# A decoder trunk on one core: each dense product in seven block products, all tokens per stage

## The chip, the cores and the metric

One core of a Trainium2 chip (trn2) runs the whole program. The metric is device time in microseconds (us) of one execution; lower is better. The engines are TensorE (PE in the rows; PEld is its loading of weights), VectorE (DVE), ScalarE (ACT), Pool (GpSimd) and SyncE (SP), which issues every DMA in one queue.

## The reference, cut to what matters

The stream x has 1024 tokens of 1024 features, in float32. Layer 0 mixes tokens by a Conformer convolution, layer 1 by causal differential attention with 8 heads; both are followed by a gated FFN with a hidden width of 2816 and a causal convolution of width 3. Every sub-layer is wrapped in RMS norms and in shift, scale and gate vectors that are computed from c.

```python
u = h @ w1 + b1;  a, gt = split(u);  u = a * sigmoid(gt)             # layer 0
u = causal_dwconv(u, dw, dwb)                                        # 31 taps
y = silu(layer_norm(u)) @ w2 + b2
s = q @ k.T * scale + bias;  p = softmax(s)                          # layer 1, two maps a head
y = rms_norm((p[0] - lam * p[1]) @ v) @ w_o
u = causal_dwconv(h @ w_in, ffn_dw, ffn_dwb);  g, v = split(u)       # FFN, 3 taps
y = (silu(g) * v) @ w_out
x = x + gate * rms_norm(y)                                           # after each sub-layer
```

The dense products are w1 (1024 x 2048), w2, w_q, w_k, w_v, w_o (1024 x 1024 each), and for each of two FFNs w_in (1024 x 5632) and w_out (2816 x 1024).

## The kernel before, in words

Every operand of a product is kept as two float32r tiles, hi (the value rounded to float32r) and lo (what the rounding left), and a product of a 128 x 128 block is three matmuls: hi x hi, hi x lo, lo x hi. `featmm` (L206 to L214) gives a tile of 128 features by 512 tokens; `tokmm` (L216 to L251) gives four tiles of 128 tokens by 512 columns. `wsplit` (L173 to L193) loads a weight tile of 128 x 1024, copies hi on ScalarE (L191) and subtracts lo (L192), on Pool by a share that `plan['pool']` sets, otherwise on VectorE.

The 1024 tokens are worked in two halves, A and B, of 512. A planner written by hand, `interleave` (L72), runs one generator of the other half's work beside the steps of an FFN:

- The convolution of half A has its own time: 7 of 31 taps go through TensorE as products with a diagonal (L468), 24 are instructions of VectorE on PSUM (L473). The convolution of half B runs beside the FFN of half A (`interleave` at L645).
- Attention of half A (`attn`, L742 to L862) runs beside the FFN of layer 0 of half B (L919), and attention of half B beside the FFN of layer 1 of half A (L934).
- Residual sums, norms and transposes of one half (`residual` L299, `transposing` L275) are placed beside products of the other.

`ffn` (L389) makes w_in's products chunk by chunk, takes three taps from PSUM (L402, L405, L406), the gate (L415, L416), the operands (L168, L169), and after each of three parts of the hidden width adds w_out's products into y (L427). The activations between the two products stay in SBUF. The modulation vectors are 96 dot products of loaded tiles of 128 x 1024 (`mod_dot`, L341 to L345). In attention, each tile of 128 queries and each of two maps has scores (L788), bias and maximum on VectorE (L793, L800, L804), the exponential on ScalarE (L805), then the two maps are combined (L807 to L810), transposed (L827), rounded (L829, L830) and multiplied with V (L836 to L838); squares for the norm follow (L843 to L858).

Order within an engine is that of its queue. Tile buffers rotate in pools, and a load of a tile waits in SP's queue until a buffer is free, with all later DMAs behind it.

## Time and profile before

| | us |
|---|---|
| Two runs | 2617.18 and 2612.99, median 2615.09 |
| Profiled execution, first to last instruction (span) | 2617.6 |

The profile gives no time of its own execution beside the span. It names an engine, a line, an operation and tiles as output <- inputs. A busy time is that of a group of instructions, where an overlap counts once; a mean is that of one instruction. A matmul's own duration overlaps with the next one's, so TensorE's pace is read from the number of matmuls in a stretch. The granted clock is given as a share of 2.4 GHz.

### The profile page before, as it was taken

How to read it: one execution, taken by the hardware profiler on the slowest of the kernel's cores; microseconds unless marked ns; L12 is line 12 of the kernel's file. 1: busy time of each engine (PE TensorE's matmuls, PEld its weight loads, DVE VectorE, ACT ScalarE, POOL GpSimd, SP SyncE). 2: the span in 40 equal slices, each digit the busy share in tenths (PEclk: the TensorE clock that was granted, in tenths of full speed). 3: DMA queues.
4: the chain of work that ended last, by engine and by line, in shares of the span. 5: the costliest groups of instructions: out<-in, count | busy, mean ns of one | idle time of the engine just before them, and what ended most of it. 6: DMA issues, size and time to landing. Idle time of an engine off the chain costs nothing.

```text
span 2617.6 us, 30604 instructions
## 1 busy us (share of the span) xinstructions
PE 2442.6 (93%) x10678; PEld 1923.3 (73%) x10678; DVE 1768.1 (68%) x3289; ACT 1160.1 (44%) x1883; POOL 921.0 (35%) x487
## 2 busy tenths in 40 slices
PE   6998889999989979999999999999999998999997
PEld 4666667777767767787787778777777776788885
DVE  6998689999788438747667844775676665624335
ACT  4433234332444225647554533655664544433333
POOL 2234334544644322222222333323323334344443
PEclk9999989999999989999999999999999999999999
DMA  7123753443335877444453486445445324433332
GB/s 279 57 65 99 208 183 96 142 141 120 105 111 181 266 200 218 137 133 137 127 163 105 138 290 200 141 120 136 119 129 137 120 84 158 161 97 91 95 97 73
DMA packets 161898, 370.31 MB, mean 141 GB/s; under 512 B 21712, under 2 KB 70224, under 8 KB 161744
## 3 DMA queue, kind: packets, MB, share of 16 engines
q1 hardware_dynamic: 161744, 368.36, 46.0%
q8 instruction: 85, 1.39, 0.2%
q14 instruction: 69, 0.57, 0.1%
HBM read 320.56 MB, written 47.73 MB: 141 GB/s over the span
## 4 chain that ended last, share of the span: by engine, by line
PE 44%; DVE 14%; DMA 3%; issue 3%; ACT 2%; POOL 1%; SPq 0%; DVEq 0%; ACTq 0%; POOLq 0%
PE Pu L214 8%; PE Pu L212 8%; PE Pu L213 8%; PE Py L228 5%; PE Py L229 5%; PE Py L227 5%; PE Psc L788 2%; DMA mraw<-in_mw_dram 2%; DVE tap L405 1%; DVE p L810 1%; DVE tap L406 1%; DVE gT L169 1%; POOL wlo L192 1%; PE Ptr L827 1%; DVE tap L416 1%
## 5 line engine op out<-in xcount | busy, mean ns | idle before, releaser
L192 POOL TENSOR_TENSOR wlo<-raw,whi 128x1024 fp32r<-128x1024 f32 x344 | 843.7, 2453 | 1539.9 <-ACT whi L191 1453.7
L191 ACT CAST whi<-raw 128x1024 fp32r<-128x1024 f32 x374 | 392.2, 1049 | 665.2 <-issue 310.5
L212 PE MATMUL Pu<-hT,whi 128*128 128x512 f32 x1536 | 616.9, 402 | 18.5 <-DVE tap L406 11.1
L214 PE MATMUL Pu<-hT,wlo 128*128 128x512 f32 x1536 | 611.7, 398 | 3.2 <-POOL wlo L192 3.2
L213 PE MATMUL Pu<-hT,whi 128*128 128x512 f32 x1536 | 611.1, 398 | 1.0 <-DVE hT L290 0.9
L227 PE MATMUL Py<-whi,gT 128*128 128x512 f32 x960 | 387.2, 404 | 31.5 <-DVE hl L689 14.2
L228 PE MATMUL Py<-wlo,gT 128*128 128x512 f32 x960 | 385.0, 401 | 4.7 <-POOL wlo L192 4.6
L229 PE MATMUL Py<-whi,gT 128*128 128x512 f32 x960 | 383.5, 399 | 0.5 <-DVE gT L169 0.5
L212 PEld LDWEIGHTS Pu<-hT,whi 128*128 128x128 f32 x1536 | 291.5, 190 | 89.8 <-issue 15.9
L214 PEld LDWEIGHTS Pu<-hT,wlo 128*128 128x128 f32 x1536 | 291.3, 190 | 70.6 <-POOL wlo L192 5.2
L213 PEld LDWEIGHTS Pu<-hT,whi 128*128 128x128 f32 x1536 | 291.4, 190 | 65.8 <-DVE hT L290 2.4
L473 DVE SCALAR_TENSOR_TENSOR Pcv<-cu,sv,Pcv 128x512 f32<-128x512 f32 x432 | 299.7, 747 | 3.4 <-PE Pcv L468 2.5
L405 DVE SCALAR_TENSOR_TENSOR tap<-Pu,sv,tap 128x511 f32<-128x511 f32 x176 | 131.1, 745 | 199.8 <-ACT tap L402 169.8
L227 PEld LDWEIGHTS Py<-whi,gT 128*128 128x128 f32 x960 | 183.8, 191 | 75.6 <-issue 17.1
L228 PEld LDWEIGHTS Py<-wlo,gT 128*128 128x128 f32 x960 | 183.7, 191 | 47.7 <-POOL wlo L192 8.1
L229 PEld LDWEIGHTS Py<-whi,gT 128*128 128x128 f32 x960 | 183.4, 191 | 42.6 <-DVE gT L169 1.0
L345 DVE CUSTOM_DVE_ANT_0 mraw<-mraw,crow 128x1024 f32<-128x1024 f32 x96 | 147.5, 1538 | 74.1 <-DMA mraw<-in_mw_dram 74.0
L402 ACT ACTIVATE tap<-Pu,sv 128x512 f32<-128x512 f32 x176 | 136.2, 774 | 4.3 <-PE Pu L214 4.3
L406 DVE SCALAR_TENSOR_TENSOR tap<-Pu,sv,tap 128x510 f32<-128x510 f32 x176 | 130.9, 744 | 2.6
L168 ACT CAST gT<-tap 128x512 fp32r<-128x512 f32 x88 | 54.5, 619 | 162.2 <-DVE tap L416 162.0
L805 ACT ACTIVATE p<-p,sm 128x128 f32<-128x128 f32 (+7 forms) x128 | 99.2, 775 | 49.8 <-DVE sm L804 48.7
L169 DVE TENSOR_TENSOR gT<-tap,gT 128x512 fp32r<-128x512 f32 x88 | 89.5, 1018 | 31.6 <-ACT gT L168 31.0
(213 smaller groups left out, 3377.9 us busy)
## 6 DMA issues: line engine op xcount, KB each, us to landing
raw<-in_win_dram SPq DMA_DIRECT2D x176, 512.0 KB, 3.7
mraw<-in_mw_dram SPq DMA_DIRECT2D x96, 512.0 KB, 4.6
raw<-in_wout_dram SPq DMA_DIRECT2D x88, 512.0 KB, 3.7
raw<-in_w_dram SPq DMA_DIRECT2D x48, 512.0 KB, 3.7
Q<-qd SPq DMA_DIRECT2D x128, 128.0 KB, 3.3
K<-kd SPq DMA_DIRECT2D x48, 256.0 KB, 4.6
V<-vd SPq DMA_DIRECT2D x192, 64.0 KB, 2.0
xt<-xd SPq DMA_DIRECT2D x20, 512.0 KB, 4.9
```

The costliest lines, as they stand in the source:

```text
L191: A.copy(hi, raw)
L192: e.tensor_tensor(out=lo, in0=raw, in1=hi.bitcast(F32), op=ALU.subtract)
L212: T.matmul(ps, lhsT=a, rhs=ah, start=(k == 0), stop=False)
L213: T.matmul(ps, lhsT=a, rhs=al, start=False, stop=False)
L214: T.matmul(ps, lhsT=b, rhs=ah, start=False, stop=(k == KC - 1))
L227: T.matmul(ps[t], lhsT=a, rhs=rh, start=(f == 0), stop=False)
L228: T.matmul(ps[t], lhsT=a, rhs=rl, start=False, stop=False)
L229: T.matmul(ps[t], lhsT=b, rhs=rh, start=False, stop=(f == n - 1))
L345: V.tensor_tensor_reduce(out=raw, in0=raw, in1=crow, scale=1.0, scalar=0.0, op0=ALU.mult, op1=ALU.add, accum_out=r[:, k:k + 1])
L405: V.scalar_tensor_tensor(out=t[:, 1:512], in0=ps[:, 0:511], scalar=w[1], in1=t[:, 1:512], op0=ALU.mult, op1=ALU.add)
L406: V.scalar_tensor_tensor(out=t[:, 2:512], in0=ps[:, 0:510], scalar=w[0], in1=t[:, 2:512], op0=ALU.mult, op1=ALU.add)
L473: V.scalar_tensor_tensor(out=ps, in0=u[:, j:j + 512], scalar=col("dw", j * 8 + c), in1=ps, op0=ALU.mult, op1=ALU.add)
```

## The change

Each dense product C = A B is cut into 2 x 2 blocks and made from seven block products, of sums and differences of blocks of A and of B, with additions of the results. All 1024 tokens go through a stage before the next begins: the two halves of the tokens are the two block columns, so there is no second half to interleave with.

- `Feat` makes products that end with features on the partitions (w1, w_in, w_k, w_q). A step (q, p) is one of seven products for a pair of chunks q: `prep` forms its block of weights (four sums S per pair) and the hi and lo of it, `step` has 12 matmuls of 512 columns and one addition or copy of the result, and `ahead` prepares five steps early. Two steps of each of the first two pairs need the first token half alone and are made early. `w_k` and `w_q` are scaled, so that Q, K and V share one set of operands; Q's shift becomes a bias (`q_bias`).
- `token_stage` makes products that end with tokens on the partitions (w2, w_v, w_o, w_out). A step loads one block of activations and one of weights from HBM, 256 KB each, and splits each into hi and lo (`loaded`); in w_v the activations are the operands already there.
- Activations between two products and the sums of their blocks are stored in HBM (`prep_s`), as are sums of weight blocks (`prep_t`, `prep_v`).
- `eng` sends a share of the sums and subtractions to Pool: 0.9 in the convolution, 0.3 in `Feat`, 0.25 elsewhere.
- `operands_2` makes the operands' block sums once the second token half is there.
- The convolution (31 taps on 1024 tokens per chunk) runs in w1's stage: 7 taps on TensorE, 5 on ScalarE and Pool, 19 on VectorE. LayerNorm follows by itself, then w2.
- Attention runs by itself, both halves one after the other, between w_q and w_o. K, V and Q come in two sets of buffers, and PSUM is one pool of 8 banks.
- A `Ticker` spreads other work over the steps: the FFN's taps and gate, `prep_s` and `prep_t`, and the modulation vectors, 48 of whose dots go along with the down-projection of layer 0.

The core of the diff:

```diff
-P1, P2, P3, P4 = 1, 1, 0.7, 1      # share of the weights' lo parts made by Pool: convolution, Q/K/V, the two attention phases
-AE, BE = 52, 52      # FFN steps that attention goes along with, first and second half
...
+FEAT = (1, 6, 2, 5, 7, 3, 4)
+TOK = (1, 6, 2, 5, 3, 7, 4)
+BANK = {1: 0, 2: 0, 6: 1, 5: 2, 3: 2, 7: 3, 4: 3}
+OPEN = (1, 6, 5, 7)
+NHS, NWS, NSS, NQ = 56, 12, 6, 12
+LA = 5
+LAT = 4
...
+    def tick(self, n=1):
+        n += len(self.q) > 1
+        while n > 0 and self.q:
+            if next(self.q[0], "end") == "end":
+                self.q.popleft()
+            else:
+                n -= 1
...
+    def eng():
+        plan["debt"] += plan["pool"]
+        if plan["debt"] >= 1.0:
+            plan["debt"] -= 1.0
+            return G
+        return V
...
+    def operands_2(xn, scale, shift, H, Z):
+        for kp in range(4):
+            z = Z[kp]
+            zz = [s2("zz"), s2("zz")]
+            for two in range(2):
+                k = 2 * kp + two
+                ps = bank("Pt")
+                for t in range(4):
+                    T.transpose(ps[:, t * P:(t + 1) * P], xn[4 + t][:, k * P:(k + 1) * P], ident)
+                scaled(zz[two], ps, scale, shift, k)
+            def put(i, src):
+                pr = hpair()
+                split(*pr, src, eng())
+                H[i].append(pr)
+            sub(half(z, 0), zz[0], half(z, 0))
+            sub(zz[0], zz[1], zz[0])
+            put(3, zz[1])
+            sub(zz[1], zz[1], half(z, 0))
+            put(6, zz[1])
+            sub(half(z, 1), half(z, 1), zz[1])
+            put(5, half(z, 0))
+            put(7, zz[0])
+            put(4, half(z, 1))
+            yield
...
+        def __init__(self, n, src, H, done, ticks=1, scale=None):
+            self.n, self.src, self.H, self.done, self.ticks, self.scale = n, src, H, done, ticks, scale
+            e = min(EARLY, n)
+            self.steps = [(q, p) for p in (1, 2) for q in range(e)]
+            self.early = len(self.steps)
+            self.steps += [(q, p) for q in range(e) for p in FEAT if p not in (1, 2)]
+            self.steps += [(q, p) for q in range(e, n) for p in FEAT]
+            self.raw, self.sums, self.pairs, self.banks, self.outs = {}, {}, {}, {}, {}
+            self.at, self.made = 0, 0
...
+        def prep(self, q, p):
+            def a1(i):
+                return self.rawof(q, 0)[:, i]
+            def a2(i):
...
+            def s(n):
+                if n not in su:
+                    t = None
+                    if n == 1:
+                        t = s2("S")
+                        add(v4(t), a2(0), a2(1), eng())
+                    elif n == 2:
+                        a = s(1)
+                        t = s2("S")
+                        sub(v4(t), a, a1(0), eng())
+                    elif n == 3:
+                        t = s2("S")
+                        sub(v4(t), a1(0), a2(0), eng())
+                    else:
+                        a = s(2)
...
+            src = {1: lambda: a1(0), 2: lambda: a1(1), 3: lambda: s(4), 4: lambda: a2(1), 5: lambda: s(1), 6: lambda: s(2),
+                   7: lambda: s(3)}[p]()
+            hi, lo = wpair()
+            A.copy(v4(hi), src)
+            eng().tensor_tensor(out=v4(lo), in0=src, in1=v4(hi).bitcast(F32), op=ALU.subtract)
+            self.pairs[q, p] = hi, lo
...
+        def step(self):
+            q, p = self.steps[self.at]
+            hi, lo = self.pairs.pop((q, p))
+            b = BANK[p]
+            if p in OPEN:
+                self.banks[q, b] = bank("Pf")
+            ps = self.banks[q, b]
+            for j in range(4):
+                ah, al = self.H[p][j]
+                w, v = hi[:, j * P:(j + 1) * P], lo[:, j * P:(j + 1) * P]
+                more = {"skip_group_check": True} if b != 1 else {}
+                T.matmul(ps, lhsT=w, rhs=ah, start=(p in OPEN and j == 0), stop=False, **more)
+                T.matmul(ps, lhsT=w, rhs=al, start=False, stop=False, **more)
+                T.matmul(ps, lhsT=v, rhs=ah, start=False, stop=(j == 3), **more)
+            if p == 1:
+                self.outs[q] = [q4("X"), None]
+            o = self.outs[q]
+            if p == 6:
+                o[1] = q4("Y")
+            X, Y = o
+            if p == 1:
+                A.copy(half(X, 1), ps)
+            elif p == 6:
+                add(half(Y, 0), ps, half(X, 1))
+            elif p == 2:
+                A.copy(half(X, 0), ps)
+            elif p == 5:
+                add(half(Y, 1), ps, half(Y, 0))
+            elif p == 7:
+                add(half(Y, 1), ps, half(Y, 1))
+            elif p == 3:
+                add(half(X, 1), ps, half(Y, 0))
+            else:
+                add(half(Y, 0), ps, half(Y, 0))
+                self.tk.add(self.done(q, X, Y))
+            self.at += 1
...
+        def rest(self):
+            while self.at < len(self.steps):
+                self.ahead(self.at + 1 + LA)
+                self.step()
+                self.tk.tick(self.ticks)
+            self.tk.flush()
...
+    def prep_t(wsrc, dst, e=None):
+        u, v = q4("tu"), q4("tv")
+        dma(out=u, in_=wsrc(0))
+        dma(out=v, in_=wsrc(1))
+        yield
+        sub(half(u, 0), half(v, 0), half(u, 0), eng())
+        yield
+        sub(half(v, 0), half(v, 1), half(v, 0), eng())
+        yield
+        sub(half(v, 1), half(v, 1), half(u, 0), eng())
+        yield
+        sub(half(u, 1), half(u, 1), half(v, 1), eng())
+        dma(out=dst[0], in_=u)
+        dma(out=dst[1], in_=v)
...
+    def prep_s(g0, g1, dst):
+        dma(out=dst[0][:, 0:512], in_=half(g0, 0))
+        dma(out=dst[1], in_=g1)
+        a, b = s2("S"), s2("S")
...
+    def loaded(src, mk):
+        r = w2k("raw")
+        dma(out=r, in_=src)
+        pr = mk()
+        split(*pr, r, eng())
+        return pr
...
+        def ahead(upto):
+            while made[0] < min(upto, len(steps)):
+                p, j = steps[made[0]]
+                have[p, j] = asrc(p, j), bsrc(p, j)
+                made[0] += 1
...
+        def mm(p, j, t, ps):
+            (ah, al), (bh, bl) = have[p, j]
+            a, b = ah[:, t * P:(t + 1) * P], al[:, t * P:(t + 1) * P]
+            more = {"skip_group_check": True} if p != 6 else {}
+            T.matmul(ps[t], lhsT=a, rhs=bh, start=(p in OPEN and j == 0), stop=False, **more)
+            T.matmul(ps[t], lhsT=a, rhs=bl, start=False, stop=False, **more)
+            T.matmul(ps[t], lhsT=b, rhs=bh, start=False, stop=(j == n - 1), **more)
...
+        k = 0
+        for p in TOK:
+            if p in OPEN:
+                banks[BANK[p]] = [bank("Py") for _ in range(4)]
+            ps = banks[BANK[p]]
+            jm = n - late if p == TOK[-1] else n
+            for j in range(jm):
+                ahead(k + 1 + LAT)
+                for t in range(4):
+                    mm(p, j, t, ps)
+                have.pop((p, j))
+                k += 1
+                tk.tick(ticks)
+            if jm == n:
+                for t in range(4):
+                    evac(p, t, ps[t])
+            else:
+                ahead(len(steps))
+                for t in range(4):
+                    for j in range(jm, n):
+                        mm(p, j, t, ps)
+                    evac(p, t, ps[t])
+                    tk.tick(ticks)
...
+        def pre(t, nh):
+            a = half(y[t], nh)
+            if bt is not None:
+                add(a, a, bt[nh])
+            square(a, ss2[:, nh * 8 + t:nh * 8 + t + 1])
+            eng().tensor_tensor(out=a, in0=a, in1=gn[nh], op=ALU.mult)
+            yield
...
+        token_stage(n, asrc, bsrc, lambda t, nh: half(y[t], nh), fin, Both(), ticks, late=late)
+        tk.flush()
+        after.flush()
+        if nxt is not None:
+            if nxt[3] is not None:
+                nxt[3].begin()
+            drain(operands_2(y, nxt[0], nxt[1], nxt[2], Z))
...
+        onpe = list(range(0, NPE))
+        onpool = list(range(NPE, NPE + NPOOL))
+        onv = list(range(NPE + NPOOL, CW))
+        for d in onpe:
+            dg = big.tile([P, P], F32, tag="dg", bufs=3, name=nm("dg"))
+            A.activation(dg, ident, AF.Copy, scale=w(d))
+            last = d == onpe[-1]
+            T.matmul(ps[0][:, d:512], lhsT=dg, rhs=X[:, 0:512 - d], start=(d == 0), stop=last)
+            T.matmul(ps[1], lhsT=dg, rhs=X[:, 512 - d:1024 - d], start=(d == 0), stop=last)
...
+        def done(q, X, Y):
+            ts = []
+            for ch, src in ((q, X), (q + FC, Y)):
+                w = [col("fdw", (l * 3 + j) * 44 + ch) for j in range(3)]
+                t = q4("tap")
+                A.activation(t, src, AF.Identity, bias=col("fdwb", l * 44 + ch), scale=w[2])
+                yield
+                V.scalar_tensor_tensor(out=t[:, 1:], in0=src[:, 0:1023], scalar=w[1], in1=t[:, 1:], op0=ALU.mult, op1=ALU.add)
+                V.scalar_tensor_tensor(out=t[:, 2:], in0=src[:, 0:1022], scalar=w[0], in1=t[:, 2:], op0=ALU.mult, op1=ALU.add)
+                yield
+                ts.append(t)
+            tg, tv = ts
+            A.activation(tg, tg, AF.Silu)
+            yield
+            V.tensor_tensor(out=tv, in0=tg, in1=tv, op=ALU.mult)
+            if q % 2 == 0:
+                G0[q] = tv
+                yield from prep_t(lambda nh: wout[l, nh, q // 2], td[q // 2])
+            else:
+                yield from prep_s(G0.pop(q - 1), tv, ad[q // 2])
+        f = Feat(FC, lambda q: (win[l, q], win[l, q + FC]), H, done)
...
+    for g in (mod_scale(1, 1, 0, s_m1), mod_col(1, 0, sh_m1), gate_row(1, 2, 1, gd_m1), mod_scale(1, 4, 2, s_f1),
+              mod_col(1, 3, sh_f1), gate_row(1, 5, 3, gd_f1), *[prep_v(j) for j in range(4)],
+              *[prep_t(lambda nh, j=j: wo[nh, j], wot[j]) for j in range(4)]):
+        tk.add(g)
+    with_residual(FC // 2, fa0, fb0, gd_f0, lambda t: xd[0][t], lambda t: xd[1][t], (None, None, H, fk), tk, late=6)
+    plan["pool"] = WPOOL
+    fk.tk.add(strips())
+    fk.tk.add(q_bias())
+    fk.rest()
...
+    token_stage(4, lambda p, j: H[p][j], lambda p, j: loaded(sblock(wva[j], p), wpair), lambda t, nh: half(vy[t], nh), v_fin, vt,
+                transposed=True)
...
+    fq.begin_ahead()
+    fq.begin()
+    vt.flush()
+    fq.rest()
+    hopen.close()
...
+    drain(attn(0))
+    wo_norm(0)
+    drain(attn(1))
+    wo_norm(1)
...
+    for j in range(4):
+        drain(prep_s(wo_act(2 * j), wo_act(2 * j + 1), woa[j]))
+    aopen.close()
...
+    f1, fa1, fb1 = ffn(1, H)
+    with_residual(4, lambda p, j: loaded(sblock(woa[j], p), hpair), tok_weights(lambda nh, j: wo[nh, j], wot), gd_m1,
+                  lambda t: xd[1][t], lambda t: xd[2][t], (s_f1, sh_f1, H, f1), Ticker())
+    plan["pool"] = WPOOL
+    f1.rest()
+    plan["pool"] = TPOOL
+    with_residual(FC // 2, fa1, fb1, gd_f1, lambda t: xd[2][t], lambda t: out[t], None, Ticker(), late=6)
```

## Rows read from the trace of the kernel before

**Rows 1.** The page, busy time of each engine, share of the span, instructions.
```profile
PE 2442.6 (93%) x10678; PEld 1923.3 (73%) x10678; DVE 1768.1 (68%) x3289; ACT 1160.1 (44%) x1883; POOL 921.0 (35%) x487
```

**Rows 2.** The page, chain of work that ended last, by engine.
```profile
PE 44%; DVE 14%; DMA 3%; issue 3%; ACT 2%; POOL 1%; SPq 0%; DVEq 0%; ACTq 0%; POOLq 0%
```

**Rows 3.** Busy time by stretch: length, busy (instructions), clock, DMA share, GB/s.
```profile
130.00:196.00 66.00, 66.00 (x238) 44.45 (x237) 63.52 (x97) 23.11 (x49) 22.93 (x11) 1.00 0.22 64
...
1113.00:1178.00 65.00, 64.36 (x303) 52.08 (x302) 30.95 (x101) 30.47 (x63) 17.24 (x13) 1.00 0.49 134
...
2356.00:2421.00 65.00, 65.00 (x281) 52.69 (x281) 27.47 (x50) 23.00 (x29) 28.68 (x12) 1.00 0.30 90
```

**Rows 4.** Groups of instructions: busy us, mean ns, idle before and releaser.
```profile
L192 POOL TENSOR_TENSOR wlo<-raw,whi 128x1024 fp32r<-128x1024 f32 x344 | 843.7, 2453 | 1539.9 <-ACT whi L191 1453.7 <-DMA V<-vd 14.1 <-PE Pu L213 13.8
L212 PE MATMUL Pu<-hT,whi 128*128 128x512 f32 x1536 | 616.9, 402 | 18.5 <-DVE tap L406 11.1 <-DVE hT L289 1.9 <-ACT c L477 1.9
...
L473 DVE SCALAR_TENSOR_TENSOR Pcv<-cu,sv,Pcv 128x512 f32<-128x512 f32 x432 | 299.7, 747 | 3.4 <-PE Pcv L468 2.5
...
L345 DVE CUSTOM_DVE_ANT_0 mraw<-mraw,crow 128x1024 f32<-128x1024 f32 x96 | 147.5, 1538 | 74.1 <-DMA mraw<-in_mw_dram 74.0
...
L169 DVE TENSOR_TENSOR gT<-tap,gT 128x512 fp32r<-128x512 f32 x88 | 89.5, 1018 | 31.6 <-ACT gT L168 31.0
...
L287 ACT ACTIVATE hf<-Pm,mod,mod 128x512 f32<-128x512 f32 x64 | 49.3, 778 | 48.3 <-PE Pm L281 18.1 <-DVE mod L349 13.6 <-DVE mod L352 6.7
...
L427 DVE TENSOR_TENSOR yf<-Py,yf 128x512 f32<-128x512 f32 x72 | 48.3, 687 | 58.9 <-PE Py L229 58.7
```

**Rows 5.** Timeline: start us, us, engine and line; four undisturbed instructions.
```profile
7.04 1.06 ACT L259 ACTIVATE junk<-ym 128x1024 bf16<-128x1024 f32 x1 [0.72 <-DMA ym<-in_x_dram]
...
8.33 1.06 ACT L259 ACTIVATE junk<-ym 128x1024 bf16<-128x1024 f32 x1
...
36.03 1.22 DVE L345 CUSTOM_DVE_ANT_0 mraw<-mraw,crow 128x1024 f32<-128x1024 f32 x1
...
1915.85 1.27 DVE L810 SCALAR_TENSOR_TENSOR p<-p,sm,p 128x1024 f32<-128x1024 f32 x1
```

**Rows 6.** Timeline: VectorE beside Pool's subtraction, at the start and in the convolution.
```profile
15.93 2.34 POOL L192 TENSOR_TENSOR wlo<-raw,whi 128x1024 fp32r<-128x1024 f32 x1 [13.57 <-ACT whi L191]
15.96 2.32 DVE L162 TENSOR_TENSOR sm<-sm 128x4 f32<-128x4 f32 x1
...
18.32 0.16 DVE L163 SCALAR_TENSOR_TENSOR sm<-sm,sm 128x4 f32<-128x4 f32 x1
...
147.25 5.36 DVE L473 SCALAR_TENSOR_TENSOR Pcv<-cu,sv,Pcv 128x512 f32<-128x512 f32 x8
147.85 2.41 POOL L192 TENSOR_TENSOR wlo<-raw,whi 128x1024 fp32r<-128x1024 f32 x1 [4.98 <-ACT whi L191]
```

**Rows 7.** DMA issues: count, KB each, median us from issue to landing.
```profile
mraw<-in_mw_dram SPq DMA_DIRECT2D x96, 512.0 KB, 4.6
raw<-in_wout_dram SPq DMA_DIRECT2D x88, 512.0 KB, 3.7
```

**Rows 8.** Busy time by stretch, as rows 3: two stretches of many loads.
```profile
916.00:982.00 66.00, 51.78 (x229) 41.90 (x228) 24.27 (x35) 16.59 (x22) 19.43 (x8) 0.90 0.73 201
...
1505.00:1571.00 66.00, 63.93 (x274) 51.02 (x274) 32.53 (x61) 21.65 (x31) 20.14 (x10) 1.00 0.88 291
```

**Rows 9.** Groups of instructions, as rows 4: attention on VectorE and ScalarE.
```profile
L805 ACT ACTIVATE p<-p,sm 128x128 f32<-128x128 f32 (+7 forms) x128 | 99.2, 775 | 49.8 <-DVE sm L804 48.7
...
L810 DVE SCALAR_TENSOR_TENSOR p<-p,sm,p 128x128 f32<-128x128 f32 (+3 forms) x64 | 64.8, 1013 | 1.2
L793 DVE CUSTOM_DVE_ANT_0 p<-Psc,rb 128x512 f32<-128x512 f32 (+3 forms) x128 | 63.7, 504 | 32.1 <-PE Psc L788 29.9
...
L804 DVE TENSOR_REDUCE sm<-sm 128x1 f32<-128x2 f32 (+2 forms) x128 | 19.4, 152 | 2.7
L846 DVE TENSOR_TENSOR sh<-sq,sh 128x256 fp32r<-128x256 f32 x32 | 19.1, 596 | 40.9 <-ACT sh L845 40.3
```

More of the change, by code (lines that the diff above doesn't have):

```diff
@@ L2 @@
 import math
+from collections import deque
 from contextlib import ExitStack
@@ L161, in newton @@
         for _ in range(3):
[L162 to L169 removed]
+            V.tensor_tensor(out=t, in0=y, in1=y, op=ALU.mult)
@@ L732, in trunk @@
[L732 to L743 removed]
+        lmt = q4("lmt")
@@ L748, in attn @@
[L748 to L754 removed]
+            K = [q4("K", F32R), q4("K", F32R)]
```

1124 lines of the change are left out of this document (502 added, 622 removed).

## The prediction

> **What bounds the kernel now.** I read the engine totals first. TensorE is busy in 93% of the span and VectorE in 68% [rows 1]; the chain that ended last lies on TensorE for 44%, more than three times its share on any other engine [rows 2]. So the bound is TensorE, with VectorE second. Next the stretches. In one where only FFN products run, TensorE issues 281 matmuls in 65 us without a pause: 65 / 281 = 0.2313 us for one matmul of 512 columns [rows 3]. In the stretch from 1113 us, which holds attention, TensorE is busy 64.4 of 65 us and VectorE 31.0 [rows 3]: attention's vector work costs almost no time there, because FFN matmuls of the other half run beside it. In the first half's convolution VectorE is busy 63.5 of 66 us and TensorE's 238 instructions hide behind it (the stretch from 130 us [rows 3]). The product matmuls are 9024 (lines 212 to 214 and 227 to 229; the largest group, of L212, has 1536 [rows 4]): 9024 x 0.2313 = 2087 of the 2617.6 us. The rest is mostly matmuls of attention and convolution.
>
> The profile gives one span, 2617.6 us, and nothing around it; it is 0.1% above the median 2615.09 of the runs, so I compare the sum with either. 2% of the time, about 52 us, is what a measurement of this kernel can tell from no change.
>
> **What the change gives.** Seven products for eight: 9024 x 7/8 = 7896 matmuls, 1128 fewer, 261 us if TensorE were the bound everywhere.
>
> **What it takes.** Every stage now handles all 1024 tokens before the next begins. So convolution and attention lose the FFN matmuls that covered them, and nothing fills TensorE between stages. And each product brings additions, mostly on VectorE. I therefore add up the stages, each by the engine that ends last in it.
>
> Prices, in us. A 512-column tensor-tensor 0.69 (L427 [rows 4]); a 1024-column one with two inputs in SBUF 1.27, by the undisturbed instruction [rows 5]; a convolution tap 0.694 (299.7 / 432 [rows 4]); a modulation dot 1.3 undisturbed (1.22 and a short read [rows 5]) and 1.54 as measured on average [rows 4]. A Pool subtraction of 1024 columns takes 2.4 [rows 4, 6], so 1.2 for 512.
>
> **The lock between Pool and VectorE.** An instruction of four columns on VectorE, 0.16 us as a rule, took 2.32 us beside a Pool subtraction of 2.34, and both ended together [rows 6]. Eight convolution taps, which read PSUM and SBUF, took 5.36 us across another Pool subtraction, no longer than without [rows 6]. So sums that move to Pool stop VectorE's own two-SBUF instructions rather than running beside them, and only PSUM readings pass. The Trainium skill's page "SBUF — State Buffer" (section "SBUF: two separate sides") says the same: the port pair is locked by one of the two for a whole instruction. By that rule the FFN's up-projections come to 20.5 us a step as below; by a free Pool they would be bound by TensorE at 19.4, some 48 us less in all.
>
> **Stage by stage.**
>
> 1. Start, 87 us. Eight x tiles land, eight squares follow each other at 1.29, the first at 7.04 us [rows 5]: 17; statistics and two dots 5; eight normalisations 5.5; 14 dots at 1.3, 18: 46. Before, this ran beside the first products. Then the first half's operands (eight scalings at 0.78 [rows 4] and their rounded copies on ScalarE, a little less each), 11, and the second half's: per pair of chunks five sums and five subtractions, ten at 0.69 = 6.9, four pairs 28, with Pool's share 30. TensorE has only early products beside this.
>
> 2. w1 and convolution, 290. Per chunk VectorE has 38 taps x 0.694 = 26.4, five additions from PSUM 3.4, gate 1.3, two last additions 1.4, its tenth of the eleven sums 0.8, one dot 1.5: 34.8. TensorE has 84 x 0.2313 = 19.4 and 28 tap matmuls, less. 8 x 34.8 = 279, and 11 for the first chunk's products.
>
> 3. LayerNorm, 65, now alone: 16 centrings, 16 products and 16 block sums at 0.69 = 33; two Newton roots of 11 instructions 15; the convolution's result stored and read back, 3.7 each way as loads land [rows 7]; waits for SiLU and the first operands 9.
>
> 4. w2, 145: 28 steps of 12 matmuls 78; 16 dots, two in each early step, 14; the last residual rows 25 (two pairs, each four residual instructions 3, two gates and a normalisation 3, 24 small ones 4, waits for the squares 2.5); operands 28.
>
> 5. FFN 0 up, 461. Per pair of chunks: 11 sums and subtractions for weights (four sums, seven low parts), four for w_out and the activations. Of the 13 that the planner shares, 3.9 go to Pool; VectorE keeps 11.1 x 0.69 = 7.7, five additions from PSUM 3.4, four taps of 1024 at 1.27 = 5.1, one product 1.2: 17.4. Pool's 3.9 x 1.2 = 4.7 hold it up except for the fifth that reads PSUM: +3.8 = 21.2, less up to 1.2 where instructions overlap as the taps do (0.747 each, 0.694 a piece). I take 20.5 against TensorE's 19.4; ends 19.4 and 22.5. 22 x 20.5 = 451, and eight dots 10. L169's 1.018 where L427 has 0.687 [rows 4] is the same hold-up in the kernel before.
>
> 6. FFN 0 down, 312: 77 steps x 2.78 = 214; the last chunk through HBM 10; in the first 24 steps two modulation dots each, 3.1 on VectorE, with 1.0 of subtractions, 0.6 of Pool's lock and 0.2 of additions 4.9 a step for 2.78, at most 50, and I take 45 (ends 0 and 60: the loads, 1.6 MB a step, would need 320 GB/s, and the busiest stretch moved 291 at a share of 0.88 [rows 8]); last rows 15; operands 28.
>
> 7. K, V, Q, 255: 3 x 336 x 0.2313 = 233; bias products and strips in K 17; hand-overs 5.
>
> 8. Attention alone, 400. Seven of its VectorE groups, from L793's 63.7 to L846's 19.1, sum to 306 [rows 9]. The small ones not shown (416 or so, at L804's 0.152) are an estimate of 62. L810 averages 1.013 where 1024 undisturbed columns take 1.27, so some 20 of the sum is Pool's lock, which goes: 340 is the floor, if VectorE never waits. Each of 64 query tiles also has a reciprocal behind an exponential of 0.775 [rows 9], 50 in all; 32 pairs end in a chain transpose, copy, subtraction, product, square, 3.5 us each if nothing fills it, 112. Ends 340 and 490; 400, since the order is set by the planner's readiness and fills some.
>
> 9. Head norms and w_o's operands 45 (16 scalings at a tap's 0.75, 16 sums, a Newton root 8, two landings). w_o 133: 80 + 25 + 28.
>
> 10. FFN 1 up 451, down 239 (214 + 10 + 15).
>
> Sum: 87 + 290 + 65 + 145 + 461 + 312 + 255 + 400 + 45 + 133 + 451 + 239 = **2883 us**, 10% slower. Of the loss against 2617.6, attention without cover (400) and the boundaries outweigh the 261 saved.
>
> **Rivals.**
>
> *TensorE stays the bound.* The mechanism is that VectorE's additions stay under TensorE's time in every product stage, and early products and readiness order cover the boundaries. For it: 93% busy now, and VectorE has 32% free over the span. Against: its time in up-projection, 17.4 alone, is within 2 us of 19.4 before Pool's lock. It decides at 19.4 us of VectorE and Pool per pair. Floors: start 75, convolution 280, LayerNorm 50, w2 113, FFN 0 427 + 259, K/V/Q 238, attention 340, head norms 30, w_o 113, FFN 1 427 + 226 = 2578. That is 1.5% below the kernel before: not slower. 0.12, of which 0.05 is faster by over 2%, where a stage still overlaps the next.
>
> *Loads starve the token stages.* Each step of w2, V, w_o and the down-projections needs two loads of 256 KB, on one SP queue behind stores and modulation loads that wait for buffers. If a step took 4.0 instead of 2.78, 238 steps cost 290 more: 2883 + 290 = 3173. For it: modulation loads land after 4.6 us [rows 7], and in a stretch of such loads TensorE fell to 51.8 of 66 us [rows 8]. Against: four steps of lead are 11 us, and 0.52 MB per 2.78 us is 189 GB/s of the 291 seen. 0.15.
>
> *The products aren't cut,* because a matmul of a block runs slower. Same shape of 128 x 128 by 512: I give it no chance of its own.
>
> **How the numbers follow.** The forecast, 2883, has 0.73; starvation 0.15; TensorE's bound 0.12. The forecast's unknown ends are attention -60/+90, each up-projection -24/+44, the dots -45/+15, boundaries +-60: taken partly together, 2700 to 3070. Starvation need not be whole, and so the range goes to 3090; below, it goes to 2690 and leaves the floor out. Faster by over 2%: 0.05; within 2%: 0.07; slower: 0.88.
>
> **What would show it.** Right: 7896 product matmuls; TensorE's share near 75% and VectorE's over 80%; in the up-projections VectorE full and TensorE waiting for its subtractions, some 20.5 us per pair; attention 400 us with TensorE half idle; gaps of 40 to 55 us of TensorE at each of the four changes of operands; a granted clock below 1.00 there, as in the row at 0.90 where TensorE waits [rows 8]. Wrong: an up-projection at 19.4 us with VectorE idle, attention under 350, or token stages far above 2.78 us a step with SP's queue as the one waited for. If TensorE's clock stays at half, 1.2 of 2.4 GHz, through attention, that stage would be longer than its range.

## The result, and the profile after

The changed kernel takes 3296.49 us (two runs, 3294.82 and 3298.16) against 2615.09: a ratio of 1.2603, 95% interval [1.2566, 1.2639]. The forecast was slower, but 2883, and the range ended at 3090. The profiled execution has a span of 3293.0 us.

First the page of the changed kernel: the engine totals, which answer to [rows 1], and the 40 slices for TensorE and its granted clock.

```profile
PE 2435.6 (74%) x9804; PEld 1882.4 (57%) x9804; DVE 2357.5 (72%) x3945; ACT 1230.5 (37%) x2169; POOL 789.4 (24%) x570
...
PE   2666744838899987688488855555558599999998
...
PEclk8788977968999999899699865577779799999999
```

TensorE falls from 93% to 74% of a longer span, VectorE rises from 68% to only 72%. Nothing is full over the span, so the added time is mostly waiting. The slices show where: the first nine (start, convolution, LayerNorm, w2) and the row of 5s (attention and the head norms), where the clock stands lowest too.

The stages, in us, each from its first matmul in TensorE's timeline to the first of the next (a down-projection from the up-projection's last matmul, attention to its own last). A stage includes its tail up to the first product that needs the second token half.

| stage | forecast | measured |
|---|---|---|
| start, w1 and convolution | 87 + 290 = 377 | 512.3 |
| LayerNorm | 65 | 36.4 |
| w2 | 145 | 189.5 |
| FFN 0 up | 461 | 472.9 |
| FFN 0 down | 312 | 394.6 |
| K, V, Q | 255 | 111.9 + 90.8 + 108.7 = 311.4 |
| attention | 400 | 503.7 |
| head norms | 45 | 31.4 |
| w_o | 133 | 150.5 |
| FFN 1 up | 451 | 463.5 |
| FFN 1 down | 239 | 226.8 |

The differences are +135, -29, +45, +12, +83, +56, +104, -14, +18, +13 and -12, in all +410. Convolution, attention and FFN 0's down-projection are 322 of it.

Busy time by stretch of the changed kernel (columns as in [rows 3]): an up-projection, a down-projection, and attention in two stretches of about equal length (the scores of the second token half begin at 2113 us).

```profile
2670.00:2740.00 70.00, 65.47 (x287) 53.08 (x286) 63.78 (x72) 29.82 (x43) 22.52 (x13) 1.00 0.43 158
3090.00:3160.00 70.00, 70.00 (x311) 57.98 (x310) 49.10 (x58) 44.87 (x77) 25.22 (x18) 1.00 0.84 292
...
1917.00:2170.00 253.00, 140.89 (x523) 110.48 (x524) 141.12 (x569) 86.86 (x251) 5.89 (x34) 0.55 0.42 115
2170.00:2420.00 250.00, 141.60 (x693) 120.29 (x692) 149.41 (x498) 92.05 (x198) 4.51 (x26) 0.73 0.34 88
```

A product matmul still costs what it did: 70 / 311 = 0.2251 us against 0.2313 [rows 3]. So the seven-for-eight cut is real, and FFN 1's down-projection, where nothing else rides along, comes out as forecast. In attention VectorE is busy 141.12 + 149.41 = 290.5 of 503 us and ScalarE 179: no engine is the bound. The clock of 0.55 is nearly all the lower of its two levels, 1.2 of 2.4 GHz, in a stretch where TensorE stops and waits after every few matmuls.

What TensorE waited for in the whole changed kernel (us in total, times, longest):

```profile
PE Ptr L1027 <- DVE p L1011: 172.2, 57, 5.8
PE Pf L379 <- ACT wh L355: 132.8, 13, 24.2
PE Pf L379 <- DVE Y L194: 86.8, 52, 15.0
PE Pcv L669 <- DVE X L657: 74.4, 5, 22.2
PE Py L503 <- ACT hh L187: 71.0, 40, 12.4
```

The rows name attention (the transpose waits for the combined maps), the convolution (weights, additions and gate) and the operands of the token stages. The largest wait comes 57 times at some 3 us: a chain, not one late transfer.

### The profile page after: what moved, and what is told of

The parts are those of the page before. It is cut to its first block, busy times and chain, and to the rows that moved or that the text cites. A ratio compares the mean times of both kernels' runs of the same rounds, so it can differ in the third digit from the quotient of the medians.

```text
span 3293.0 us, 31668 instructions
## 1 busy us (share of the span) xinstructions
PE 2435.6 (74%) x9804; PEld 1882.4 (57%) x9804; DVE 2357.5 (72%) x3945; ACT 1230.5 (37%) x2169; POOL 789.4 (24%) x570
## 5 line engine op out<-in xcount | busy, mean ns | idle before, releaser
L379 PE MATMUL Pf<-hh,wh 128*128 128x512 f32 x1680 | 696.1, 415 | 233.4 <-ACT wh L355 132.8
L381 PE MATMUL Pf<-hh,wl 128*128 128x512 f32 x1680 | 676.7, 403 | 11.8 <-POOL wl L356 9.6
L380 PE MATMUL Pf<-hl,wh 128*128 128x512 f32 x1680 | 677.8, 404 | 9.9 <-POOL hl L188 9.2
L379 PEld LDWEIGHTS Pf<-hh,wh 128*128 128x128 f32 x1680 | 329.4, 196 | 336.4 <-ACT wh L355 139.4
L503 PE MATMUL Py<-hh,hh 128*128 128x512 f32 x840 | 324.8, 409 | 76.2 <-ACT hh L187 71.0
L504 PE MATMUL Py<-hl,hh 128*128 128x512 f32 x840 | 346.6, 413 | 45.0 <-DVE hl L188 26.4
L381 PEld LDWEIGHTS Pf<-hh,wl 128*128 128x128 f32 x1680 | 328.5, 196 | 89.3 <-POOL wl L356 12.8
L380 PEld LDWEIGHTS Pf<-hl,wh 128*128 128x128 f32 x1680 | 329.7, 196 | 86.5 <-POOL hl L188 12.4
L505 PE MATMUL Py<-hh,hl 128*128 128x512 f32 x840 | 339.9, 405 | 0.0
L188 DVE TENSOR_TENSOR hl<-raw,hh 128x512 fp32r<-128x512 f32 x311 | 256.7, 856 | 103.4 <-ACT hh L187 75.9
L1027 PE MATMUL Ptr<-ident,p 128*128 128x128 f32 x288 | 77.9, 410 | 172.2 <-DVE p L1011 172.2
```

The costliest lines, as they stand in the source:

```text
L188: (e or V).tensor_tensor(out=lo, in0=src, in1=hi.bitcast(F32), op=ALU.subtract)
L379: T.matmul(ps, lhsT=w, rhs=ah, start=(p in OPEN and j == 0), stop=False, **more)
L380: T.matmul(ps, lhsT=w, rhs=al, start=False, stop=False, **more)
L381: T.matmul(ps, lhsT=v, rhs=ah, start=False, stop=(j == 3), **more)
L503: T.matmul(ps[t], lhsT=a, rhs=bh, start=(p in OPEN and j == 0), stop=False, **more)
L504: T.matmul(ps[t], lhsT=a, rhs=bl, start=False, stop=False, **more)
```

## The experiments

Every edit is against the changed kernel unless it says otherwise; a long one is cut to its core. Most kernels ran once. In those that leave a stage alone its length still varies: start with convolution 512 to 519 us, attention 502 to 506, FFN 0's down-projection 391 to 399.

**1. Two heads in lockstep.**

```diff
-    drain(attn(0))
+    def both(hf):
+        g = [attn(hf, range(0, NH, 2)), attn(hf, range(1, NH, 2))]
+        while g:
+            g = [x for x in g if next(x, "end") != "end"]
+
+    both(0)
     wo_norm(0)
-    drain(attn(1))
+    both(1)
```

`attn` takes the list of its heads, and there are half as many buffers more for what the heads keep (p, ah, al, BT, sh; Q in a set of its own).

> Two heads of attention go in lockstep, so that while one head waits in its chain (scores, maximum, exponential, combining, transpose, copy, product with V) the other has work in the queues. Nothing is left out. Theory (attention is set by that chain, one head at a time): the stretch from the last Q product to the last product with V, 503 us in the changed kernel, falls to about 400 (nearer VectorE's 340), and the time to about 3195. Rival (the low granted clock of 0.50 to 0.74 there, or VectorE's own work, sets it): under 30 us less, about 3270 or more.

3178.67 us; attention 383.7 instead of 503.7. The stage in this kernel in two stretches:

```profile
1922.00:2115.00 193.00, 113.53 (x514) 94.86 (x514) 128.97 (x573) 84.50 (x248) 5.63 (x32) 0.71 0.55 152
2115.00:2306.00 191.00, 123.76 (x704) 107.06 (x704) 146.62 (x499) 95.04 (x202) 4.52 (x26) 0.79 0.45 115
```

Nearly the same VectorE work (275.6 us busy, from 290.5) in 120 us less, and TensorE's waits for the combined maps fall from 172.2 us to 57.4: the chain of one head had set the stage. The clock rises from 0.55 and 0.73 without any added matmul, while TensorE waits less.

**2. The same buffers, heads one after the other.** Only the buffer sizes of experiment 1, as

```diff
-                        p = at.tile([P, 1024], F32, tag="p", bufs=6, name=nm("p"))
+                        p = at.tile([P, 1024], F32, tag="p", bufs=9, name=nm("p"))
```

> The larger buffer sets of the run with two heads in lockstep, but heads one after the other as in the changed kernel; nothing is left out. If the planner would fill one head's waits with the next head by itself, and only buffers held it back, attention falls from 504 us towards 384. If it doesn't look that far ahead, attention stays within 20 us of 504.

3301.36 us, attention 503.7: nothing. The planner here is the ordering of the queues when the program is built (the `interleave` of the kernel before has no part in it). In the changed kernel it draws the next head's first scores forward, among the products with V of the head before,

```profile
1941.15 1.06 PE L989 MATMUL Psc<-K,Q 128*128 128x256 f32 x4
```

and larger buffers add nothing to that; the source has to put more there.

**3. Matmuls that only fill.**

```diff
+    fill = bank("Pfill")
...
+                        for _ in range(6):
+                            T.matmul(fill[:, 0:256], lhsT=half(Q[c], 0)[:, tl * P:(tl + 1) * P], rhs=K[c][:, 0:256], start=True, stop=True)
```

> After the scores of each map six more matmuls of 256 columns go into a PSUM bank that nobody reads, to keep TensorE busy and its clock up; nothing is left out. There are 128 maps, so 768 matmuls, about 0.11 us each at the full clock: 85 us of TensorE. Rival (the low granted clock sets attention's 503 us): the granted clock there rises towards 1.00 and the stage shortens by 50 us or more. Theory (the chain through VectorE and ScalarE sets it): the clock rises, and the stage stays within 20 us of 503, or grows by part of the 85.

3262.59 us, attention 475.6. By stretch:

```profile
1921.00:2160.00 239.00, 180.99 (x1089) 162.78 (x1088) 149.17 (x607) 93.43 (x263) 6.25 (x36) 0.84 0.48 129
2160.00:2396.00 236.00, 164.35 (x898) 145.56 (x897) 140.62 (x462) 86.61 (x186) 4.16 (x24) 0.76 0.33 87
```

More work, 28 us less time, between both expectations. The granted clock went from 0.55 to 0.84 in the first stretch. So part of attention's length is the low clock, which itself comes with the waits.

**4. Both.** The edits of experiments 1 and 3 together.

> Two heads in lockstep, and six more matmuls of 256 columns after each map's scores into a bank that nobody reads; nothing is left out. If the clock (0.71 and 0.79 in attention with two heads) still costs time beside the chain, attention falls from 384 us by 15 or more; if with two heads VectorE and the chain alone set it, it stays at 384 or grows by part of the 85 us of added matmuls.

Attention 369.4 (383.7 with two heads alone), time 3167.20: 14 us, just under the bound set. The clock's share shrinks once the chain is filled.

**5. Nothing to Pool outside the convolution.**

```diff
-WPOOL = 0.3
+WPOOL = 0.0
-TPOOL = 0.25
+TPOOL = 0.0
```

> No sums and subtractions go to Pool outside the convolution's stage; nothing is left out. Theory (a subtraction on Pool stops VectorE for its length, so a share on Pool gives nothing): VectorE has 13 x 0.69 + 3.4 + 5.1 + 1.2 = 18.7 us per pair plus small ones, and an up-projection stays within 15 us of 473 and 463. Rival (Pool runs beside VectorE): an up-projection grows by 3.9 x 0.69 = 2.7 us per pair, 22 pairs, about 60 us each.

3168.97 us: 128 less, where at most 15 a stage was expected. The up-projections take 421.3 and 414.1 (from 472.9 and 463.5), w2 178.9, FFN 0 down 380.3, w_o 145.4. The dearest group in FFN 0's up-projection on VectorE and on Pool, in the changed kernel (columns as [rows 4]):

```profile
L356 DVE TENSOR_TENSOR wl<-S,wh 128x512 fp32r<-128x512 f32 x51 | 47.3, 927 | 1.8 <-ACT wh L355 1.2
...
L356 POOL TENSOR_TENSOR wl<-S,wh 128x512 fp32r<-128x512 f32 x29 | 43.8, 1514 | 121.9 <-ACT wh L355 91.4 <-PE Pf L381 19.7 <-PE Pf L380 8.9
```

And the group on VectorE without Pool, with a stretch of FFN 1's up-projection in that kernel:

```profile
L356 DVE TENSOR_TENSOR wl<-S,wh 128x512 fp32r<-128x512 f32 x80 | 54.7, 683 | 2.1 <-ACT wh L355 2.1
...
2600.00:2670.00 70.00, 70.00 (x310) 57.96 (x309) 66.29 (x91) 32.08 (x45) 0.00 (x0) 1.00 0.46 169
```

One subtraction takes Pool 1.51 us and VectorE 0.683, and beside Pool VectorE's own take 0.927. With all of them on VectorE, it does 91 instructions in 66.29 of 70 us, where it did 72 in 63.78 in the stretch from 2670 us above, and TensorE is busy all 70: 414.1 / 22 = 18.8 us a pair is TensorE's pace (84 x 0.2251 = 18.9). What TensorE waited for in FFN 0's up-projection of the changed kernel was additions in VectorE's queue,

```profile
PE Pf L379 <- DVE Y L194: 32.2, 23, 3.1
```

and hardly Pool's own results (1.5 us); without Pool this row is gone. The lock was read rightly in [rows 6]; that sharing then costs more than it relieves was not worked out. The Trainium skill's page "SBUF — State Buffer" (section "SBUF: two separate sides") has the pair held by one engine for a whole instruction while the other blocks; the 0.927 against 0.683 agrees.

**6. Gate and first taps issued at once; 7. all weight sums to Pool.** Experiment 6 runs four steps of the convolution's generator at the last product of a chunk:

```diff
-                self.tk.add(self.done(q, X, Y))
+                g = self.done(q, X, Y)
+                if self.done.__name__ == "conv":
+                    for _ in range(4):
+                        next(g, None)
+                self.tk.add(g)
```

Experiment 7:

```diff
-CPOOL = 0.9
+CPOOL = 1.0
```

> In the convolution a chunk's gate, and the first of its tap products on TensorE, are issued as soon as the chunk's products are done, not after the next product step. Nothing is left out. Theory (a chunk costs 47.8 us instead of the forecast 34.8 because its gate stands in VectorE's queue, TensorE's taps wait for the gate, and VectorE's taps wait for TensorE's, all adding into the same PSUM bank): a chunk falls by 4 to 8 us, the stage of 396 us by 30 to 60. Rival (VectorE's own work, or weights that wait for it, sets the chunk): within 15 us of 396.

> In the convolution's stage all sums and low parts of weights go to Pool, none to VectorE, where one in ten went to VectorE behind a queue of taps. Nothing is left out. Theory (TensorE starves there, 132.8 us on the high and 86.8 us on sums in the whole kernel, mostly for weights that stand behind taps in VectorE's queue): the stage of 396 us falls by 30 us or more. Rival (the order of gate and taps within a chunk sets it): within 15 us of 396.

3302.57 and 3293.28 us; start with convolution 519.5 and 517.0 against 512.3. Both theories fell: neither stage is shorter. In experiment 6 the waits for the gate went from 74.4 us to 50.9, and the stage didn't gain. So I read a chunk's timeline. VectorE in the changed kernel, from a chunk's gate to its second group of taps (start, length; the wait before in brackets):

```profile
324.43 3.05 DVE L657 SCALAR_TENSOR_TENSOR X<-X,sv,Y 128x1024 f32<-128x1024 f32 x1
339.21 0.69 DVE L194 TENSOR_TENSOR Y<-Pf,Y 128x512 f32<-128x512 f32 x1 [11.73 <-PE Pf L381]
345.38 0.69 DVE L194 TENSOR_TENSOR Y<-Pf,Y 128x512 f32<-128x512 f32 x1 [5.47 <-PE Pf L381]
346.23 1.52 DVE L680 SCALAR_TENSOR_TENSOR Pcv<-X,sv,Pcv 128x500 f32<-128x500 f32 x2 [0.16 <-PE Pcv L669]
```

TensorE beside it, and busy time by stretch around it:

```profile
327.63 2.05 PE L669 MATMUL Pcv<-X,dg 128*128 128x512 f32 x2 [21.58 <-DVE X L657]
...
331.12 1.02 PE L669 MATMUL Pcv<-X,dg 128*128 128x511 f32 x2
331.98 1.02 PE L670 MATMUL Pcv<-X,dg 128*128 128x512 f32 x2
...
312.50:326.00 13.50, 0.00 (x0) 0.00 (x0) 13.50 (x20) 1.14 (x2) 4.43 (x3) 0.50 0.10 36
326.00:346.50 20.50, 18.87 (x53) 10.42 (x53) 3.14 (x4) 9.99 (x16) 17.51 (x12) 0.88 0.08 28
```

The two engines take turns. While VectorE adds its taps TensorE does nothing (13.5 us and more, 21.58 by its own wait); then TensorE adds its seven taps into both banks, with the products of two steps among them, and VectorE does nothing for 17.4 of 20.5 us. From 331.12 to 331.98 a tap's half is 0.86 us; after the long idle, in which the granted clock stood at 0.50, the first cost double.

**8. Taps by halves of the tokens.**

```diff
-        for d in onpe:
-            ...
-            T.matmul(ps[0][:, d:512], lhsT=dg, rhs=X[:, 0:512 - d], start=(d == 0), stop=last)
-            T.matmul(ps[1], lhsT=dg, rhs=X[:, 512 - d:1024 - d], start=(d == 0), stop=last)
+        for h in range(2):
+            for d in onpe:
+                ...
```

The same for VectorE's taps. The order of the sum within a bank stays.

> In the convolution, TensorE's 7 taps and VectorE's 19 go through the first 512 tokens, then through the second, so that VectorE may begin on the first bank while TensorE works on the second; before, both banks went along tap by tap. Nothing is left out; seven more small copies on ScalarE make the diagonals a second time. Theory (VectorE stands idle for the 18 us in which TensorE adds its taps into both banks): the wait falls to about half, a chunk by some 8 us, and start with convolution from 512 us to 450 to 465. Rival (the weights of the next products, not the taps, set the chunk): within 15 us of 512.

3229.64 us; start with convolution 449.2, 63 less. The waits of VectorE in this stage, in the changed kernel:

```profile
DVE Y L194 <- PE Pf L381: 66.9, 10, 11.7
...
DVE Pcv L680 <- PE Pcv L669: 15.3, 5, 13.7
```

and by halves:

```profile
DVE Y L194 <- PE Pf L381: 14.7, 10, 9.8
...
DVE Pcv L683 <- PE Pcv L671: 9.5, 4, 7.1
```

82 us of waits become 24. The wait is named after a product's addition, because that stands first in VectorE's queue behind TensorE's taps; the cause is the taps. The last chunks show it best. The gate of the fifth chunk in the changed kernel is that at 324.43 above, and this is the eighth:

```profile
468.61 1.27 DVE L657 SCALAR_TENSOR_TENSOR X<-X,sv,Y 128x1024 f32<-128x1024 f32 x1
```

The same two gates by halves:

```profile
304.36 1.27 DVE L657 SCALAR_TENSOR_TENSOR X<-X,sv,Y 128x1024 f32<-128x1024 f32 x1
...
407.65 1.27 DVE L657 SCALAR_TENSOR_TENSOR X<-X,sv,Y 128x1024 f32<-128x1024 f32 x1
```

A chunk takes (468.61 - 324.43) / 3 = 48.1 us in the one and (407.65 - 304.36) / 3 = 34.4 in the other, where the forecast had 34.8.

**9. Two taps on TensorE instead of seven.**

```diff
-NPE, NPOOL = 7, 5
+NPE, NPOOL = 2, 5
```

> Two taps on TensorE and 24 on VectorE instead of 7 and 19; nothing is left out. Theory (the taps of the two engines follow one another, since they add into the same banks): five taps cost 5 x 4 x 0.43 = 8.6 us less on TensorE, with products that ran between them up to 14, and 5 x 1.3 = 6.5 us more on VectorE; a chunk changes by -8 to -2 us, start with convolution by -60 to -15. Rival (VectorE's work alone sets the chunk): it grows by 8 x 6.5 = 52 us.

3283.76 us; start with convolution 502.4, 10 less than the changed kernel, whose 512.3 is the lowest of 512 to 519: a little short of the theory and far from the rival's +52. From the fifth gate to the eighth a chunk takes 42.2 us instead of 48.1. So 8 x 6.5 = 52 us more of VectorE's taps are more than paid for by TensorE's shorter turn.

**10. The modulation dots in FFN 0's down-projection, taken apart.** Four kernels make a square: loads and dots, dots alone (on a row in SBUF), loads alone (one column copied), neither.

```diff
+        if l == 1:
+            V.tensor_tensor_reduce(out=raw, in0=crow, in1=crow, scale=1.0, scalar=0.0, op0=ALU.mult, op1=ALU.add,
+                                   accum_out=r[:, k:k + 1])
+            return
```

That is the one with dots alone, ahead of the load; the one with loads alone has, behind the load, and the one with neither, ahead of it with crow for raw:

```diff
+        if l == 1:
+            V.tensor_copy(r[:, k:k + 1], raw[:, 0:1])
+            return
```

> The 48 modulation dots of layer 1, which go along with the down-projection of layer 0, read a row that is in SBUF already; their loads of 512 KB each are left out, VectorE's work stays. What is left out: the modulation weights of layer 1 don't enter the result. Theory (the loads hold that stage up: DMA share 0.9 to 1.0 until about 1475 us): it falls from 395 us to 320 to 345. Rival (VectorE's 48 dots at 1.3 or more, ahead of the operands' subtractions, hold it up): it stays above 370.

> The 48 modulation dots of layer 1 are left out, loads and VectorE's work both; a copy of one column stands in for each. The modulation of layer 1 is so left out of the result. Theory (loads): the down-projection of layer 0 falls from 395 us to the same 320 to 345 as without the loads alone. Rival (VectorE's work): only this run falls by more than 40 us.

> The 48 dots of layer 1 keep their loads of 512 KB, but VectorE copies one column of each instead of the dot. What is left out: the dots of layer 1, so its modulation. In the down-projection of layer 0, 395 us in the changed kernel, the loads alone gave 19 when left out and loads and dots together 88. If VectorE's work carries the rest by itself, this run falls by about 69, to 326; if loads and dots cover one another, by clearly less, and the stage stays above 350.

The stage takes 394.6 with both (3296.49 us), 375.9 with the dots alone (3275.01), 397.0 with the loads alone (3296.48) and 306.8 with neither (3206.65). The first 100 us of the stage in each: the changed kernel,

```profile
1211.00:1311.00 100.00, 74.33 (x278) 52.12 (x276) 83.16 (x126) 32.08 (x52) 22.51 (x11) 0.91 0.94 341
```

the dots alone,

```profile
1205.00:1305.00 100.00, 81.03 (x320) 62.65 (x318) 98.72 (x144) 41.18 (x66) 33.20 (x15) 0.93 0.59 172
```

the loads alone,

```profile
1211.00:1311.00 100.00, 73.61 (x276) 51.63 (x275) 40.16 (x87) 31.07 (x50) 15.27 (x12) 0.91 0.93 332
```

and neither:

```profile
1212.00:1312.00 100.00, 97.78 (x427) 79.56 (x426) 72.23 (x85) 63.47 (x108) 29.94 (x20) 1.00 0.91 324
```

After the first two kernels I took the loads for 19 us and VectorE for the rest, 69. The third ended that: without VectorE's dots the stage is as long as before. The two are bounds that lie over one another: the loads alone hold the stage by 90 us, the dots alone by 69, and whichever is left acts. TensorE issues 278, 320, 276 and 427 matmuls. A DMA share of 0.91 to 0.94 stands in three of the four, so the share alone doesn't tell which transfers the products wait for. The waits in the same 100 us do. TensorE waits for operands' high parts (`hh`), which ScalarE makes; ScalarE's wait and SP's queue in the changed kernel,

```profile
ACT hh L187 <- DMA raw<-fa: 65.3, 20, 11.7
...
SPq L208 <- DMA mraw<-in_mw_dram: 32.9, 32, 3.8
```

ScalarE's wait with the loads alone,

```profile
ACT hh L187 <- DMA raw<-fa: 58.0, 17, 13.6
```

and SP's queue with the dots alone:

```profile
SPq L474 <- DVE hl L188: 48.4, 27, 4.2
```

With the loads, the activations (`raw<-fa`) come late behind modulation loads (L208), which SP's queue holds until an earlier one has landed; with neither loads nor dots, ScalarE waits only 2.5 us for them. With the dots alone the queue stands for another reason: a load's buffer comes free with VectorE's subtraction (`hl`), and that stands behind the dots. In the source a modulation row takes one of 12 buffers, 8 of which `y` holds in this stage; whether more buffers would free the queue was not tried.

**11. Attention drained ahead of the FFN, in the kernel before.**

```diff
-    interleave(itertools.islice(f, 60), (attn(at, 0, ssqA), NAT, 0, AE),
+    drain(attn(at, 0, ssqA))
+    interleave(itertools.islice(f, 60),
```

> The kernel before, with attention of each half run to its end ahead of the FFN that it went along with, instead of between its steps. Nothing is left out. It gives the price of the lost cover alone, without the seven products. Theory (attention alone costs the length of its chain, some 500 us, of which 9024 product matmuls covered nearly all): the time before of 2615 grows by 250 to 350 us, about 2865 to 2965. Rival (attention had cost its full time before as well): it grows by less than 100.

The same for the second token half. 2622.05 us: no change. It took away only a part of the cover. TensorE's timeline in this kernel:

```profile
1041.87 1.09 PE L788 MATMUL Psc<-K,Q 128*128 128x512 f32 x4
1042.80 0.39 PE L213 MATMUL Pu<-hT,whi 128*128 128x512 f32 x1
```

FFN products still stand between the scores, although the source issues all of attention first: the ordering at build put them there, 627 between the first and last score of the first token half (1178 in the kernel before) and 898 of the second (1194). So the run prices nothing, and the cover's price is shown only by attention's 503.7 us in the changed kernel, where no FFN product stands beside it. Why the ordering draws FFN products forward here, and no more than one tile's scores of the next head in experiment 2, stays open.

**12. The causes together.** Experiments 1 and 5; then with 8; then also 32 of the 48 dots moved from FFN 0's down-projection to attention, one each round:

```diff
         while g:
             g = [x for x in g if next(x, "end") != "end"]
+            next(dots, None)
```

> Two heads in lockstep and nothing to Pool outside the convolution's stage, together; nothing is left out. If the two causes lie in different stages and add, 3296 - 120 - 129 = 3050, about 1.16 of the time before: still slower. If one feeds on the other, over 3090.

> Two heads in lockstep, nothing to Pool outside the convolution's stage, and the convolution's taps by halves, together; nothing is left out. If the three causes lie in different stages and add: 3053 - 63 = 2990. If the convolution's gain had been given back, over 3030.

> As the run with two heads, no Pool and taps by halves, and 32 of layer 1's 48 modulation dots moved from the down-projection of layer 0 to attention; nothing is left out. Theory (the dots cost there what VectorE takes for them, 69 / 48 = 1.44 us each, because the operands' subtractions stand behind them, and attention has VectorE free for 23% and more): 32 x 1.44 = 46 us less, 2944, about 1.12 of the time before. Rival (the dots lengthen attention's chain by the same): within 15 us of the run without the move, 2990.

3052.72 us, ratio 1.1642 [1.1623, 1.1661]; 2981.00 us; 2985.37 us, ratio 1.1383 [1.1363, 1.1404]. The three causes add: 3296 - 120 - 128 - 63 = 2985 against 2981. The move of the dots gains nothing: FFN 0 down falls from 380.1 to 340.2, attention grows from 385.0 to 430.9. There TensorE's waits for K's loads double, without the move

```profile
PE Psc L992 <- DMA K<-kd: 24.7, 6, 10.3
```

and with it

```profile
PE Psc L991 <- DMA K<-kd: 49.6, 12, 10.1
```

That is 25 of the 46 us; whether the rest is VectorE's 38.9 us of dots in the chain was not separated.

## Why the prediction was wrong

**The cut and the sign: right.** 7896 product matmuls at 0.2251, and attention without cover with the boundaries outweigh the saving. Even with three causes removed, the kernel is 14% slower than before; what is left was not taken apart further.

**"I therefore add up the stages, each by the engine that ends last in it": this step failed.** It holds where both engines have work queued far ahead: up-projections 472.9 and 463.5 for 461 and 451, FFN 1 down 226.8 for 239. It fails where two engines hand one tile to and fro; there a stage costs the sum of the turns.

- *Convolution, 290.* VectorE's 34.8 a chunk stood against "TensorE has 84 x 0.2313 = 19.4 and 28 tap matmuls, less." Both figures can hold and the chunk still cost 48: the taps of both engines add into the same banks, so 17 us of waiting for TensorE's turn come on top of VectorE's work. Experiment 8 gives 63 of the 135 us back; the start has 29 (TensorE's last wait for the second half's operands ends at 116 us, where 87 stood). The other 40 or so lie ahead of the fifth chunk and were not taken apart; Pool's work stayed in that stage in every run, and beside a Pool sum of 2.34 us the gate at 324.43 took 3.05 instead of 1.27.
- *Attention, 400*, "since the order is set by the planner's readiness and fills some". Across heads it fills with one tile's scores and no more (experiment 2). The 340 of VectorE was too high: its own terms make 306 + 62 - 20 = 348, and the groups add up to 340 here too, but neighbouring instructions overlap and fill 290.5. The end of 490 was too low. With two heads it is 383.7, so 120 us are the chain of one head; the clock is a part of those, as the fill shows. The prediction's last condition, a clock that stays low through attention, came true in the first stretch (0.55).
- *Dots in FFN 0 down, 45 (ends 0 and 60).* The term was worked out from VectorE's steps; the loads were an aside of 320 GB/s. They were the larger bound: 88 us with both, 90 with loads alone, at 341 and 332 GB/s where [rows 8] had moved 291 at a share of 0.88, with SP's queue held by modulation loads. The stage without either is still 306.8 for 267. Its tail behind the last product is 46 where 15 + 28 stood; the rest lies among the products (K's first 48 run there too) and was not taken apart.

**Boundaries: sizes off.** In w2's tail, from the changed kernel's VectorE and TensorE timelines:

```profile
670.83 1.41 DVE L564 SCALAR_TENSOR_TENSOR y<-y,sm,xt 128x512 f32<-128x512 f32 x2 [4.12 <-DMA xt<-in_x_dram]
673.52 0.17 DVE L173 TENSOR_SCALAR sm<-sm 128x4 f32<-128x4 f32 x1 [1.27 <-ACT junk L199]
...
680.64 3.75 PE L256 MATMUL Pt<-ident,y 128*128 128x128 f32 x15 [20.89 <-DVE y L574]
```

Residual load, square, root and normalisation follow one another, first for one token half and then for the other; from the last product (659) to the first that needs both halves (738) it is 79 us, where 25 + 28 stood. In K, V and Q "hand-overs 5" were 50 by four rows of TensorE's waits, in K's stage, up to the end of V's, and in Q's with attention's first scores:

```profile
PE Pf L379 <- ACT hh L187: 7.0, 1, 7.0
...
PE Py L503 <- ACT wh L187: 13.7, 4, 10.2
...
PE Pf L379 <- ACT wh L355: 18.4, 2, 15.2
PE Psc L989 <- DMA K<-kd: 10.9, 1, 10.9
```

Two of the rows wait for weights (`wh`) that the source begins to prepare only behind the products of the stage before; the others wait for an operand and for K's load.

**Pool's lock: right in kind, and worth more than was made of it.** 21.5 and 21.1 us a pair against 20.5 forecast; a Pool subtraction took 1.51 us, not the 1.2 that half of 2.4 gave. The weighing was against a free Pool (19.4), never against no Pool (18.8). By the prediction's own prices that is 15 x 0.69 + 9.7 = 20.1 on VectorE, already less than with Pool.

**The rivals.** TensorE's bound fell with VectorE and TensorE both waiting. "Loads starve the token stages" was right in one stage, FFN 0's down-projection: 278 matmuls in 100 us are 4.3 us a step, where the rival had put 4.0, and SP's queue stood behind modulation loads as it said. FFN 1's down-projection runs at full pace with 292 GB/s.

## What to carry to other kernels

Before a stage is priced by its busiest engine, ask whether two engines write one tile in turn and what is queued behind each wait: then the turns add, until the work is split so that each has a tile of its own (63 us here) or two independent chains run in lockstep (120 us). Work moved to an engine that locks out the one it is meant to relieve has to be compared with not moving it at all (128 us). And where leaving out one of two loads on a stage gains little, the other may be waiting behind it: measure all four corners, and read what the queue that issues the loads waits for, before naming the cause.

## What was not expected of the hardware

- TensorE's granted clock fell to 0.55 in the first 253 us of attention, where it was 1.00 beside FFN products in the kernel before [rows 3], and 768 added matmuls made the stage 28 us shorter (clock 0.84).
- After 21.58 us of waiting the first convolution tap's half took 1.84 us (327.63 to 329.47); from 331.12 on it took 0.86.
- The modulation weights' loads took a median of 7.8 us from issue to landing, against 4.6 [rows 7]; the changed kernel's row:

```profile
mraw<-in_mw_dram SPq DMA_DIRECT2D x96, 512.0 KB, 7.8
```
